# A decoder trunk on one core: the S5 branch's rotations rewritten as reflections in two wide passes

## The chip, the cores and the metric

The kernel runs on one core of a Trainium2 chip. The metric is the device time of one execution in microseconds. Three runs of the kernel before took 1174.33, 1170.13 and 1173.74 us; the median is 1173.74 us. The engines are named as the profile names them: PE is the matrix engine (PEld its weight loads), DVE the vector engine, ACT the scalar engine, POOL the GpSimd engine, SP the engine that issues most of the DMAs.

## The reference, cut to what matters

One layer of a hybrid decoder trunk: one input projection feeds three token mixers (S5, a gated MLP, a gated delta rule), each is gated and projected, the three are merged by sigmoid gates, and one output projection and a LayerNorm follow. The change is in the S5 mixer (and at the seam behind it):

```python
dt = jnp.exp(log_dt)[:, None]
mag = jnp.exp(lr * dt)
ab_r = mag * jnp.cos(li * dt)
ab_i = mag * jnp.sin(li * dt)
...
bu_r = jnp.einsum('gpc,btgc->btgp', bb_r, u)
bu_i = jnp.einsum('gpc,btgc->btgp', bb_i, u)
cum_r, cum_i, s_r, s_i = lax.associative_scan(_cplx_combine, (a_r, a_i, bu_r, bu_i), axis=1)
s_r, s_i = s_r + cum_r * h0r - cum_i * h0i, s_i + cum_r * h0i + cum_i * h0r
y = jnp.einsum('gcp,btgp->btgc', c_re, s_r) - jnp.einsum('gcp,btgp->btgc', c_im, s_i)
z = jax.nn.gelu(y + d * xa)
z = z * jax.nn.sigmoid(z @ w_glu + b_glu)
...
pa = (ya * jax.nn.silu(ga)) @ w_pa
out = (g_a * pa + g_b * pb + g_c * pc) @ w_out
```

There are 64 groups with 64 complex states each, 256 prompt tokens and 8 samples of 4 tokens.

## The kernel before, in words

All activations lie transposed, channels on the 128 partitions and the 288 tokens (256 + 32) along the free axis. A product with a weight tile of 1024x128 is 8 steps of 3 matmuls, since each fp32 operand is split into a high and a low part: a DMA brings `raw` (512 KB), ACT rounds it to `wh` (L201), DVE makes `wl = raw - wh` (the helper `tt`, L136), and PE multiplies high by high, high by low and low by high (L228). Three `raw` buffers rotate. There are 328 such tiles in the program, and they are spread over all stages.

PE's order is written out by hand: products are put in a queue of jobs, and `fill(n)` issues the next n pieces of 12 matmuls between the steps of the mixers. The results land in two PSUM buffers `mm`; a buffer is free again once a `done` function has read it. For a merge gate that reader is a Tanh on ACT into `mth` (L1036) or, for branch A, `mga` (L1063); for the projection that follows it is DVE. The other engines' order is set by the framework's scheduler; each engine runs its own list in that order, so an instruction that waits holds up everything behind it.

The S5 stage (some 365 us) runs 8 blocks of 4 tiles q. A tile is 128 complex states; `TX` is 296, since each of the 8 samples gets one more column for its initial state. For a tile, PE makes `bu` (real and imaginary part), DVE turns it by the phase of each token, a real scan with the magnitude runs over the columns, and DVE turns it back:

- `phases` makes a sine and a cosine table `sn`, `cn` for two tiles at once (one DVE sum `ph`, L1244, and six ACT functions of 512 columns, L1247 to L1251, and four small copies). The pool `s52` gives the tables two buffers, so they cover four tiles.
- `states` makes `am`, the scan's factor, on ACT (L1262, shown as the helper's line L150): a mask times the magnitude. Two buffers rotate. Each of its two turns is two products of 592 columns and two sums of 296.
- POOL copies the initial states into `z` (L1269) between the first turn and the scan (L1271), and the final states out of it (L1278, L1279).
- `turn` copies the input `u` of the next block into the layout for `bu` by 16 small DMAs on SP (`us<-uh`, `us<-ul`, L1222). `us` has one buffer; SP's list has `raw` DMAs among them.

Behind S5 stand the GLU (eight products with `zh`, `zl`), and the projections of branch A (`pa`, operands `yah`, `yal`) in turn with the gate products of branch A, three of which were made ahead.

Of the kernel before, what the change touches and what calls it, by code (L numbers as in the profile page):

```python
# [17 lines left out]
P = 128  # L18
D = 2048
KD = 16  # L20
TP = 256
# [59 lines left out]
LONG = ("ident", "m296", "iota", "iota16", "one", "mean")  # L81
# [3 lines left out]
def constants():  # L85
# [37 lines left out]
    add("mean", np.full((P, P), 1.0 / P))  # L123
# [6 lines left out]
def body(tc, A):  # L130
# [889 lines left out]
    mt3 = tc.alloc_tile_pool(name="mt3", bufs=3, side="right")  # L1020
    s5 = tc.alloc_tile_pool(name="s5", bufs=1, side="right")
# [37 lines left out]
    def merge_gate(m):  # L1059
        def done(ps):  # L1060
            gates[m] = mt3.tile([P, TT], F32, name="mga", tag="mga")
# [129 lines left out]
    class Block:  # L1191


        def __init__(self, n):
# [17 lines left out]
            nc.sync.dma_start(out=self.h0, in_=A["h0"][:, 4 * n:4 * n + 4])  # L1212
            self.cT = s52.tile([P, 4, 2, 32], F32, name="cT", tag="cT")
            nc.sync.dma_start(out=self.cT, in_=A["cT"][:, 4 * n:4 * n + 4])
            ts(self.cT[:, :, 1], self.cT[:, :, 1], -1.0)
            self.s = {}
# [20 lines left out]
        def phases(self, q):  # L1237

            ti = 4 * self.n + q
            ph = s5.tile([P, 2, TP], F32, name="ph", tag="ph")  # L1240
            pk = s5.tile([P, 2, TP], F32, name="pk", tag="pk")
            i0 = fu[:, ti:ti + 2].rearrange("p n (a o) -> p n a o", o=1).to_broadcast([P, 2, 16, 16])
            i1 = fv[:, ti:ti + 2].rearrange("p n (o b) -> p n o b", o=1).to_broadcast([P, 2, 16, 16])
# [10 lines left out]
            self.sn, self.cn = sn, cn  # L1254

        def states(self, q):
            ti = 4 * self.n + q
            bu = self.bu
            cb = mid(self.cn[:, q % 2], 2)
            sb = mid(self.sn[:, q % 2], 2)  # L1260
            am = tmp.tile([P, TX], F32, name="am", tag="s2")
            copy(am, C("m296"), mag[:, ti:ti + 1])  # L1262
# [349 lines left out]
```

## Time and profile before

| | |
|---|---|
| time, median of 3 runs | 1173.74 us |
| the profiled execution: its time, its span | 1173.79 us, 1172.0 us |
| PE busy | 1131.5 us (97%) |
| PEld busy | 1090.1 us (93%) |
| DVE busy | 905.8 us (77%) |
| ACT busy | 614.7 us (52%) |
| POOL busy | 106.7 us (9%) |
| mean granted PE clock | 0.99 |

The span runs from the first to the last instruction; the time holds 1.79 us more around it. Busy is the union of an engine's instructions; the shares are means over stages. In a timeline row the first number is the start in us, the second the duration; an entry in brackets is the idle time of the engine just before it and what ended it. Instructions on DVE overlap a little: where the next one does not depend on the last, it starts some 0.08 us before the last one's end, so the cost of one in a full queue is the distance from start to start.

### The profile page before, as it was taken

What the parts mean: (1) busy time and instruction counts of PE and PEld (TensorE: products, weight loads), DVE (VectorE), ACT (ScalarE), POOL (GpSimd) and SP (SyncE); (2) the same over time, 40 slices, a digit from 0 to 9 for tenths busy, and PEclk for the clock granted to TensorE, in tenths of its full rate; (3) what the DMA queues carried; (4) which work ended last, traced back from release to release, by engine and by line L of the source; (5) the groups of instructions that cost most, each with busy time, mean ns of one, the idle gap of its engine ahead of it and who ended that gap; (6) DMA issues with size and microseconds to landing.
All of it is one profiled execution on the core that took longest, in us unless ns stands there. A gap on an engine that the chain in (4) does not pass through costs nothing.

```text
span 1172.0 us, 25778 instructions
## 1 busy us (share of the span) xinstructions
PE 1131.5 (97%) x10380; PEld 1090.1 (93%) x10380; DVE 905.8 (77%) x1627; ACT 614.7 (52%) x1013; POOL 106.7 (9%) x232
## 2 busy tenths in 40 slices
PE   8999999999999999999999999999999999999995
PEld 7998999999999999999999899989988999999994
DVE  5778757765365989888999999999998755557775
ACT  5665455443363344485666666565653444444553
POOL 0232212100010000000111000000101000000002
PEclk9999999999999999999999999999999999999997
DMA  8553434332375775554545555555455455555552
GB/s 287 173 168 115 146 127 147 136 118 92 126 257 176 249 258 168 179 191 168 185 162 193 162 170 171 162 162 180 151 174 182 156 172 179 179 181 173 181 162 81
DMA packets 65335, 199.24 MB, mean 170 GB/s; under 512 B 10880, under 2 KB 18720, under 8 KB 65088
## 3 DMA queue, kind: packets, MB, share of 16 engines
q1 hardware_dynamic: 63696, 192.12, 49.7%
q0 software_dynamic: 1520, 5.48, 1.2%
q8 instruction: 82, 1.34, 0.5%
q14 instruction: 37, 0.30, 0.1%
HBM read 184.09 MB, written 7.84 MB: 164 GB/s over the span
## 4 chain that ended last, share of the span: by engine, by line
PE 68%; DVE 20%; issue 4%; DMA 4%; ACT 3%; SPq 1%; POOL 0%; DVEq 0%; POOLq 0%; ACTq 0%
PE mm L228 59%; DVE wl L136 7%; DVE z L136 4%; DVE u L136 2%; DVE z L1271 1%; DMA raw<-in_wst 1%; ACT wh L201 1%; PE up L599 1%; PE wp L593 1%; PE a L609 1%; PE y L1288 1%; DMA vu<-in_xT 1%; DMA s<-in_s 1%; DMA cT<-in_cT 1%; DVE ho L136 1%
## 5 line engine op out<-in xcount | busy, mean ns | idle before, releaser
L228 PE MATMUL mm<-xh,wh 128*128 128x288 f32 x1904 | 555.5, 292 | 10.0 <-ACT mth L1036 9.1
L228 PE MATMUL mm<-xh,wl 128*128 128x288 f32 x1904 | 546.0, 287 | 0.9 <-DVE wl L136 0.7
L228 PE MATMUL mm<-xl,wh 128*128 128x288 f32 x1904 | 545.9, 287 | 1.0 <-DVE xl L136 1.0
L136 DVE TENSOR_TENSOR wl<-raw,wh 128x1024 fp32r<-128x1024 f32 x328 | 400.2, 1221 | 160.9 <-ACT wh L201 157.9
L201 ACT CAST wh<-raw 128x1024 fp32r<-128x1024 f32 x328 | 341.3, 1043 | 329.2 <-PE mm L228 288.7
L228 PEld LDWEIGHTS mm<-xh,wh 128*128 128x128 f32 x1904 | 360.9, 190 | 23.8 <-ACT mth L1036 11.8
L228 PEld LDWEIGHTS mm<-xl,wh 128*128 128x128 f32 x1904 | 361.1, 190 | 1.5 <-DVE xl L136 1.2
L228 PEld LDWEIGHTS mm<-xh,wl 128*128 128x128 f32 x1904 | 361.0, 190 | 1.3 <-DVE wl L136 1.3
L228 PE MATMUL mm<-mh,wh 128*128 128x288 f32 x256 | 73.4, 287 | 0.0
L228 PE MATMUL mm<-ml,wh 128*128 128x288 f32 x256 | 73.2, 286 | 0.0
L228 PE MATMUL mm<-mh,wl 128*128 128x288 f32 x256 | 73.2, 286 | 0.0
L136 DVE TENSOR_TENSOR z<-z,u 128x296 f32<-128x296 f32 x128 | 54.9, 461 | 0.6
L1271 DVE TENSOR_TENSOR_SCAN z<-am,z 128x296 f32<-128x296 f32 x64 | 46.9, 764 | 4.4 <-POOL z L1269 2.8
L228 PEld LDWEIGHTS mm<-ml,wh 128*128 128x128 f32 x256 | 48.4, 189 | 0.1
L228 PEld LDWEIGHTS mm<-mh,wh 128*128 128x128 f32 x256 | 48.4, 189 | 0.1
L228 PEld LDWEIGHTS mm<-mh,wl 128*128 128x128 f32 x256 | 48.4, 189 | 0.0
L145 DVE SCALAR_TENSOR_TENSOR cy<-cb,convw,cy 128x312 f32<-128x312 f32 x72 | 38.6, 539 | 6.7 <-ACT cy L367 5.5
L150 ACT ACTIVATE am<-cst,mag 128x296 f32<-128x296 f32 x32 | 17.3, 542 | 47.2 <-DVE z L1271 47.2
L228 PE MATMUL mm<-yah,wh 128*128 128x288 f32 x128 | 36.7, 287 | 0.5 <-DVE yah L1381 0.5
L228 PE MATMUL mm<-ybh,wh 128*128 128x288 f32 x128 | 37.1, 290 | 0.0
L228 PE MATMUL mm<-ych,wh 128*128 128x288 f32 x128 | 37.1, 290 | 0.0
L228 PE MATMUL mm<-ybh,wl 128*128 128x288 f32 x128 | 36.7, 287 | 0.3 <-DVE wl L136 0.3
(435 smaller groups left out, 1656.5 us busy)
## 6 DMA issues: line engine op xcount, KB each, us to landing
raw<-in_wst SPq DMA_DIRECT2D x328, 512.0 KB, 3.3
s<-in_s SPq DMA_DIRECT2D x8, 512.0 KB, 6.5
out_delta_s<-s POOLq DMA_DIRECT2D x8, 512.0 KB, 3.4
us<-uh SPq DMA_DIRECT2D x64, 37.0 KB, 3.2
us<-ul SPq DMA_DIRECT2D x64, 37.0 KB, 3.2
vu<-in_xT SPq DMA_DIRECT2D x3, 576.0 KB, 7.3
out_y<-ho SPq DMA_DIRECT2D x8, 144.0 KB, 2.2
out_y<-ho SPq DMA_DIRECT2D x4, 288.0 KB, 2.5
```

What stands on the lines that cost most here:

```text
L136: (eng or V).tensor_tensor(out=out, in0=a, in1=b, op=op)
L145: V.scalar_tensor_tensor(out=out, in0=a, scalar=s, in1=b, op0=op0, op1=op1)
L150: act(out=out, in_=a, func=AF.Copy, scale=scale)
L201: S.copy(out=h, in_=r)
L228: T.matmul(pairs(ps), lhsT=w, rhs=paired(x), start=start, stop=stop)
L593: T.matmul(wp[R, h4], lhsT=xt[R, h4], rhs=r[R, h4], start=True, stop=True)
L599: T.matmul(up[:, h4], lhsT=kd[R, h4], rhs=w[R, h4], start=True, stop=True)
L609: T.matmul(a[Q, h4], lhsT=nb[R, h4, 1], rhs=w[R, h4], start=(c == 0 and h4 == 0), stop=True, skip_group_check=True)
L1271: V.tensor_tensor_scan(out=z[:, ri], data0=am, data1=z[:, ri], initial=0.0, op0=mult, op1=add)
L1288: T.matmul(self.y5[32 * q:32 * q + 32, 0:TX], lhsT=self.cT[:, q, ri], rhs=self.s[q][:, ri], start=(ri == 0), stop=(ri == 1), tile_position ...
```

## The change

- `phases` makes the tables of one tile: a sum `pk` of 256 columns, and a table `tab` with three rows: cosine, sine, minus cosine. On ACT it is two functions of 256 columns, two of 512 (both angles at once), a third Sin of 256 and one copy of 120 columns. `tab` has three buffers (pool `s53`), and `phases` is called for every tile.
- `reflect` makes both parts of a turn in two instructions: one product `pr` of 1184 columns (both parts of x, each times two neighbouring rows of `tab`), and one sum of 592. As rows (cosine, sine) and (sine, minus cosine) this is a reflection, which is its own inverse: the scan runs on the conjugate, so the imaginary part of the initial state `h0` is negated once per block (8 new small DVE instructions), and the same function turns back.
- `am` is made on POOL.
- One gate product (`merge_gate(3)`) is queued between the GLU and the first `pa`, with the pool `mt6` of six buffers for the gates from the fourth on; the gates run four ahead.
- The constant `mean` (128 columns) is gone; `one` and a scale of 1/128 in the copy take its place.

```diff
         def phases(self, q):
...
-            ph = s5.tile([P, 2, TP], F32, name="ph", tag="ph")
             pk = s5.tile([P, 2, TP], F32, name="pk", tag="pk")
-            tt(ph.rearrange("p n (a b) -> p n a b", a=16), i0, i1, add)
-            sn = s52.tile([P, 2, TX], F32, name="sn", tag="sn")
-            cn = s52.tile([P, 2, TX], F32, name="cn", tag="cn")
-            act(out=pk, in_=ph, func=AF.Abs, bias=hp[:, 1:2])
-            act(out=ph, in_=ph, func=AF.Abs)
-            for a_, tb in ((pk, sn), (ph, cn)):
-                act(out=a_, in_=a_, func=AF.Abs, bias=hp[:, 2:3])
-                act(out=tb[:, :, 0:TP], in_=a_, func=AF.Sin, scale=TURN, bias=hp[:, 3:4])
-                for i in range(2):
-                    copy(tb[:, i, TP:].rearrange("p (b t) -> p b t", t=5), mid(tb[:, i, 0:5], 8))
+            tt(pk[:, 0].rearrange("p (a b) -> p a b", a=16), i0, i1, add)
+            tab = s53.tile([P, 3, TX], F32, name="tab", tag="tab")
+            act(out=pk[:, 1], in_=pk[:, 0], func=AF.Abs, bias=hp[:, 1:2])
+            act(out=pk[:, 0], in_=pk[:, 0], func=AF.Abs)
+            act(out=pk, in_=pk, func=AF.Abs, bias=hp[:, 2:3])
+            act(out=tab[:, 0:2, 0:TP], in_=pk, func=AF.Sin, scale=TURN, bias=hp[:, 3:4])
+            act(out=tab[:, 2, 0:TP], in_=pk[:, 0], func=AF.Sin, scale=-TURN, bias=hp[:, 0:1])
+            first5 = tab[:, :, 0:5].rearrange("p k (o t) -> p k o t", o=1).to_broadcast([P, 3, 8, 5])
+            copy(tab[:, :, TP:].rearrange("p k (b t) -> p k b t", t=5), first5)
+            self.turns[q] = bass.AP(tensor=tab.tensor, offset=tab.offset, ap=[list(tab.ap[0]), [TX, 2], [TX, 2], [1, TX]])
+
+        def reflect(self, z, x, q):
+            pr = s5.tile([P, 2, 2, TX], F32, name="pr", tag="pr")
+            xb = x.rearrange("p i (o t) -> p i o t", o=1).to_broadcast([P, 2, 2, TX])
+            tt(pr, xb, self.turns[q], mult)
+            tt(z, pr[:, 0], pr[:, 1], add)

         def states(self, q):
...
-            copy(am, C("m296"), mag[:, ti:ti + 1])
+            ts(am, C("m296"), mag[:, ti:ti + 1], eng=G)
             z = s53.tile([P, 2, TX], F32, name="z", tag="z")
-            u = s5.tile([P, 2, TX], F32, name="u", tag="u")
-            tt(z, bu[:, :, 0:TX], cb, mult)
-            tt(u, bu[:, :, 0:TX], sb, mult)
-            tt(z[:, 0], z[:, 0], u[:, 1], add)
-            tt(z[:, 1], z[:, 1], u[:, 0], sub)
+            self.reflect(z, self.bu[:, :, 0:TX], q)
...
-            u = s5.tile([P, 2, TX], F32, name="u", tag="u")
-            tt(u, z, sb, mult)
-            tt(z, z, cb, mult)
-            tt(z[:, 0], z[:, 0], u[:, 1], sub)
-            tt(z[:, 1], z[:, 1], u[:, 0], add)
+            self.reflect(z, z, q)
...
-            if q == 1:
-                B.phases(2)
-            elif q == 3 and nxt:
+            if q < 3:
+                B.phases(q + 1)
+            elif nxt:
                 nxt.phases(0)
...
+    mtg.append(tc.alloc_tile_pool(name="mt6", bufs=6, side="right"))
+    merge_gate(3)
     for m in range(16):
         merge_a(m)
-        if m < 13:
-            merge_gate(m + 3)
+        if m < 12:
+            merge_gate(m + 4)
```

PE's list is the same but for one gate product (48 matmuls), which stands between the last `zh` and the first `yah` product, and the later ones that shift with it.

On DVE, the second tile of the first block, from the product that reads `bu` on (`wl` is the weight stream's instruction, `merged` a merge of another branch), before:

```order
L136 TENSOR_TENSOR z<-bu,cn 128x592
L136 TENSOR_TENSOR u<-bu,sn 128x592
L136 TENSOR_TENSOR wl<-raw,wh 128x1024
L136 TENSOR_TENSOR z<-z,u 128x296 x2
L145 SCALAR_TENSOR_TENSOR merged<-mth,mm 128x288
L1271 SCALAR_TENSOR_TENSOR z<-am,z 128x296 x2
L136 TENSOR_TENSOR wl<-raw,wh 128x1024
L136 TENSOR_TENSOR u<-z,sn 128x592
L136 TENSOR_TENSOR z<-z,cn 128x592
L136 TENSOR_TENSOR z<-z,u 128x296
L136 TENSOR_TENSOR wl<-raw,wh 128x1024
L136 TENSOR_TENSOR z<-z,u 128x296
```

The same tile on DVE now (the scan is the row with `am`):

```order
L135 TENSOR_TENSOR pr<-bu,tab 128x1184
L135 TENSOR_TENSOR wl<-raw,wh 128x1024
L135 TENSOR_TENSOR z<-pr 128x592
L144 SCALAR_TENSOR_TENSOR merged<-mth,mm 128x288
L1271 SCALAR_TENSOR_TENSOR z<-am,z 128x296 x2
L135 TENSOR_TENSOR wl<-raw,wh 128x1024
L135 TENSOR_TENSOR pr<-z,tab 128x1184
L135 TENSOR_TENSOR z<-pr 128x592
```

Eight instructions of a tile's two turns have become four; the weight stream's place among them is the same.

On ACT, in the fourth block, from the copies of `turn` to the next gate's Tanh `mth`, which frees a PSUM buffer of PE, before:

```order
L1230 CAST ws<-wtp 128x512
L1205 COPY w_6471<-bh 64x16x16 x2
L150 ACTIVATE am<-cst_143,mag 128x296
L201 CAST wh<-raw 128x1024
L1251 ACTIVATE sn<-pk,hp 128x2x256
L1251 ACTIVATE cn<-ph,hp 128x2x256
L150 ACTIVATE sn<-sn 128x40 x2
L150 ACTIVATE cn<-cn 128x40 x2
L1199 CAST bh<-bb 128x128
L201 CAST wh<-raw 128x1024
L1036 ACTIVATE mth<-mm,bgate 128x288
```

The same place on ACT now:

```order
L1231 CAST ws<-wtp 128x512
L1205 COPY w_6471<-bh 64x16x16 x2
L200 CAST wh<-raw 128x1024
L1249 ACTIVATE tab<-pk,hp 128x2x256
L1250 ACTIVATE tab<-pk,hp 128x256
L149 ACTIVATE tab<-tab 128x3x40
L200 CAST wh<-raw 128x1024
L1036 ACTIVATE mth<-mm,bgate 128x288
```

`am` is gone from the way to `mth`, and the first instruction here that needs a buffer back from DVE is the first `tab`.

On POOL, one tile's instructions now (before, the second of these rows did not exist):

```order
L1269 COPY z<-h_7477 128x2x8
L139 TENSOR_SCALAR am<-cst_143,mag 128x296
L1273 COPY sst<-z 128x2
L1274 COPY sst<-z 128x2x8
L1269 COPY z<-h_7477 128x2x8
```

Each `am` is made for the tile two ahead, so it waits for the scan of the tile whose initial states were copied just before it; the copies of the final states stand behind it.

## Rows read from the trace of the kernel before

**Rows 1.** Busy time by stage: us, PE, PEld, DVE, ACT, POOL, clock, DMA
```profile
540.00:905.00 365.00, 353.53 (x2813) 336.97 (x2812) 354.90 (x559) 218.73 (x371) 38.16 (x97) 1.00 0.52 169
905.00:945.00 40.00, 37.73 (x288) 36.89 (x288) 28.14 (x51) 16.66 (x24) 0.00 (x0) 0.96 0.49 162
```

**Rows 2.** PE's waits from 540 to 945 us: total, times, longest
```profile
PE mm L228 <- ACT mth L1036: 8.7, 9, 1.8
PE bu L228 <- DMA us<-ul: 2.6, 1, 2.6
...
PE mm L228 <- DVE yah L1381: 0.5, 1, 0.5
```

**Rows 3.** ACT's longest wait in the S5 stage
```profile
ACT am L150 <- DVE z L1271: 47.2, 26, 5.9
```

**Rows 4.** ACT's timeline before one of PE's waits: start, duration, instruction
```profile
667.04 0.54 ACT L150 ACTIVATE am<-cst,mag 128x296 f32<-128x296 f32 x1 [2.44 <-DVE z L1271]
...
668.42 0.72 ACT L1251 ACTIVATE sn<-pk,hp 128x512 f32<-128x512 f32 x1
...
670.67 1.04 ACT L201 CAST wh<-raw 128x1024 fp32r<-128x1024 f32 x1
671.62 0.49 ACT L1036 ACTIVATE mth<-mm,bgate 128x288 f32<-128x288 f32 x1
```

**Rows 5.** PE's timeline, the wait that this ended
```profile
672.16 0.39 PE L228 MATMUL mm<-xh,wh 128*128 128x288 f32 x1 [1.30 <-ACT mth L1036]
```

**Rows 6.** DVE's groups in the S5 stage: count, busy us, mean ns
```profile
L136 DVE TENSOR_TENSOR z<-z,u 128x296 f32<-128x296 f32 x128 | 54.9, 461 | 0.6
...
L136 DVE TENSOR_TENSOR z<-bu,cn 128x592 f32<-128x592 f32 x32 | 24.6, 768 | 0.1
```

**Rows 7.** DVE's timeline, a stretch without idle time
```profile
603.50 0.46 DVE L136 TENSOR_TENSOR z<-z,u 128x296 f32<-128x296 f32 x1
603.88 0.69 DVE L136 TENSOR_TENSOR ph<-fu,fv 128x512 f32<-128x512 f32 x1
604.48 1.22 DVE L136 TENSOR_TENSOR wl<-raw,wh 128x1024 fp32r<-128x1024 f32 x1
605.62 0.77 DVE L136 TENSOR_TENSOR z<-bu,cn 128x592 f32<-128x592 f32 x1
606.30 0.77 DVE L136 TENSOR_TENSOR u<-bu,sn 128x592 f32<-128x592 f32 x1
607.10 0.47 DVE L136 TENSOR_TENSOR z<-z,u 128x296 f32<-128x296 f32 x1
```

**Rows 8.** ACT's groups in the S5 stage: `am` and a table function
```profile
L150 ACT ACTIVATE am<-cst,mag 128x296 f32<-128x296 f32 x30 | 16.3, 542 | 47.2 <-DVE z L1271 47.2
...
L1251 ACT ACTIVATE sn<-pk,hp 128x512 f32<-128x512 f32 x14 | 10.1, 721 | 4.6 <-DVE u L136 4.4
```

**Rows 9.** POOL's timeline at the last tile of S5
```profile
902.00 1.12 POOL L1278 COPY sst<-z 128x2 f32<-128x2 f32 x1 [5.04 <-DVE z L136]
903.06 0.20 POOL L1279 COPY sst<-z 128x16 f32<-128x16 f32 x1
```

**Rows 10.** DVE's timeline at the same place
```profile
901.86 1.22 DVE L136 TENSOR_TENSOR wl<-raw,wh 128x1024 fp32r<-128x1024 f32 x1
```

**Rows 11.** POOL's groups over the whole span: its widest elementwise work
```profile
L136 POOL TENSOR_TENSOR ho<-ho,rsb 128x288 f32<-128x288 f32 x4 | 3.5, 912 | 253.8 <-ACT rsb L150 253.8
```

**Rows 12.** DVE's waits in the S5 stage: the one on POOL
```profile
DVE z L1271 <- POOL z L1269: 2.8, 7, 0.4
```

**Rows 13.** SP's timeline at the last block's `turn`
```profile
845.23 1.15 SPq L1222 DMA_DIRECT2D us<-uh  x2
848.17 0.33 SPq L196 DMA_DIRECT2D raw<-in_wst  x1
848.55 1.53 SPq L1222 DMA_DIRECT2D us<-ul  x2
```

**Rows 14.** Busy time by stage, the five us in which PE waits for that `us`
```profile
850.00:855.00 5.00, 2.55 (x11) 2.58 (x12) 4.90 (x9) 1.65 (x3) 1.05 (x1) 0.69 0.67 221
```

More of the change, by code (lines that the diff above doesn't have):

```diff
@@ L77, in weight_order @@
     return o
-LONG = ("ident", "m296", "iota", "iota16", "one", "mean")
+LONG = ("ident", "m296", "iota", "iota16", "one")
 _CW = {}
@@ L122, in constants @@
     add("one", np.ones((P, P)))
-    add("mean", np.full((P, P), 1.0 / P))
     return [np.ascontiguousarray(np.concatenate(x, 1)) for x in parts]
@@ L1020, in body @@
     mt3 = tc.alloc_tile_pool(name="mt3", bufs=3, side="right")
+    mtg = [mt3]
     s5 = tc.alloc_tile_pool(name="s5", bufs=1, side="right")
@@ L1060, in done @@
         def done(ps):
-            gates[m] = mt3.tile([P, TT], F32, name="mga", tag="mga")
+            gates[m] = mtg[m > 2].tile([P, TT], F32, name="mga", tag="mga")
             with tc.high_priority():
@@ L1212, in __init__ @@
             nc.sync.dma_start(out=self.h0, in_=A["h0"][:, 4 * n:4 * n + 4])
+            ts(self.h0[:, :, 1], self.h0[:, :, 1], -1.0)
             self.cT = s52.tile([P, 4, 2, 32], F32, name="cT", tag="cT")
@@ L1215, in __init__ @@
             ts(self.cT[:, :, 1], self.cT[:, :, 1], -1.0)
-            self.s = {}
+            self.s, self.turns = {}, {}
         def turn(self):
@@ L1239, in phases @@
             ti = 4 * self.n + q
-            ph = s5.tile([P, 2, TP], F32, name="ph", tag="ph")
             pk = s5.tile([P, 2, TP], F32, name="pk", tag="pk")
-            i0 = fu[:, ti:ti + 2].rearrange("p n (a o) -> p n a o", o=1).to_broadcast([P, 2, 16, 16])
-            i1 = fv[:, ti:ti + 2].rearrange("p n (o b) -> p n o b", o=1).to_broadcast([P, 2, 16, 16])
-            tt(ph.rearrange("p n (a b) -> p n a b", a=16), i0, i1, add)
-            sn = s52.tile([P, 2, TX], F32, name="sn", tag="sn")
@@ L1254, in phases @@
-            self.sn, self.cn = sn, cn
+            i0 = fu[:, ti].rearrange("p (a o) -> p a o", o=1).to_broadcast([P, 16, 16])
+            i1 = fv[:, ti].rearrange("p (o b) -> p o b", o=1).to_broadcast([P, 16, 16])
+            tt(pk[:, 0].rearrange("p (a b) -> p a b", a=16), i0, i1, add)
[3 more added lines that the diff above has]
+            act(out=pk, in_=pk, func=AF.Abs, bias=hp[:, 2:3])
@@ L1397, in merge_a @@
         queue([(("pa", m, 0), lambda k: yah[:, k], lambda k: yal[:, k])], done)
+    mtg.append(tc.alloc_tile_pool(name="mt6", bufs=6, side="right"))
+    merge_gate(3)
     for m in range(16):
         merge_a(m)
-        if m < 13:
-            merge_gate(m + 3)
+        if m < 12:
+            merge_gate(m + 4)
     drain()
+    mtg[1].release()
     mt3.release()
@@ L1454, in body @@
     sh = psl.tile([P, 512], F32, name="sh", tag="sh")
-    T.matmul(sh[:, 0:TT], lhsT=C("mean"), rhs=ho[:, 0], start=True, stop=True)
-    copy(shift, sh[:, 0:TT])
+    T.matmul(sh[:, 0:TT], lhsT=C("one"), rhs=ho[:, 0], start=True, stop=True)
+    copy(shift, sh[:, 0:TT], 1.0 / P)
     tt(ho[:, 0], ho[:, 0], shift, sub)
```

3 lines of the change are left out of this document (removed).

## Prediction

> **What bounds the kernel now.** I read the table of busy time by stage first, then who waited for whom, then the timelines around the longest waits. In the table the reader is to see that the S5 stage, 540 to 905 us, has two nearly full engines: PE 353.5 and DVE 354.9 of 365 us [rows 1]. Neither is full by itself; each loses about 11 us to the other. The stage cannot fall below PE's 353.5, since the change takes no matmul out. So the whole prize here is PE's idle time of 11.5 us, and what the clock loses beside it.
>
> PE's waits say where that time lies: 8.7 us in nine waits for `mth`, the Tanh on ACT that frees a PSUM buffer, and 2.6 us once for a small DMA of `us` [rows 2]. ACT is only 219 us busy [rows 1], so why is it late? Its longest wait is `am`, 47.2 us in 26 waits for DVE's scan [rows 3]: `am` has two buffers, and ACT's list stops there until DVE has done the scan two tiles back. One case in full: `am` starts at 667.04 after waiting 2.44 us, then come `wh`, two table functions, copies and `wh` again, and `mth` starts at 671.62 [rows 4]; PE, idle for 1.30 us by then, goes on at 672.16 [rows 5]. The chain is DVE late, ACT held, PE held. A microsecond taken from DVE's list comes back on PE as long as such waits are left, and no longer.
>
> **The change part by part.** *The turns.* Before, a tile has four products of 592 columns and four sums of 296 on DVE; the groups count 128 sums, and 32 of each product [rows 6]. Their busy means, 461 and 768 ns, overstate the cost, because neighbours overlap. From start to start, in a stretch without idle time, 296 columns took 0.38 us (603.50 to 603.88), 512 took 0.60, 1024 took 1.14 and 592 took 0.68 [rows 7]. The line through 296 and 1024 is 0.071 us + 1.044 ns a column; it gives 0.69 for 592 and 1.31 for the new 1184. One turn was 2 x 0.69 + 2 x 0.38 = 2.14 us and becomes 1.31 + 0.69 = 2.00: the columns are the same, only two fixed costs go. 64 turns give 9.1 us. If instead the busy means counted in full (1184 by the same slope 1.39 us), a turn would save 2 x 0.461 + 2 x 0.768 - 1.39 - 0.77 = 0.30, and 64 turns 19 us: the upper end. The lower end is none: the sum depends on the product just before it, and where no other instruction stands between, a dependent one starts 0.80 us after a 592 product (606.30 to 607.10) where an independent one starts after 0.68 [rows 7]; 0.12 a turn would eat nearly all of the 0.14.
>
> *The tables.* DVE now makes 32 sums of 256 columns (0.34 by the line, 10.8 us) for 16 of 512 (9.6 us): 1.2 us more. The negated `h0` is 8 instructions of 32 columns, 0.1 us each by the line, 0.8 us. Net relief of DVE: 9.1 - 1.2 - 0.8 = 7.1 us; between -2 and +17.
>
> *ACT.* From `am`'s 542 ns for 296 columns and 721 ns for 512 [rows 8], 0.83 ns a column and 0.30 us fixed: 0.51 for 256, 0.40 for 120, 0.33 for 40. A tile had three functions of 512, two small copies and `am`: 3.36 us. Now it is two of 512, three of 256 and one of 120: 3.37 us. ACT's load stays. What holds it up moves: `am` no longer stops it, but `tab` has three buffers for three tiles where `sn` and `cn` covered four, so the first `tab` of a tile waits until DVE's second product three tiles back has read its own. In the order that product is a `wl` and a product behind the scan, 1.14 + 1.31 = 2.45 us later; from there to `mth` stand 0.72, 0.51, 0.40 and a `wh` of 1.04, less some overlap, 2.3 us. Together 4.75 us from the scan's end to `mth`, against 4.58 from `am` to `mth` before [rows 4]. So ACT's path gains nothing, and the relief is DVE's alone.
>
> *`am` on POOL.* No row shows this instruction. A POOL copy of 16 columns took 0.20 us [rows 9], a two-operand instruction of 288 columns 0.91 us [rows 11]; `am` lies between, nearer the middle, 0.5 us. What does it cost DVE? POOL's copy at 902.00 took 1.12 us and ended as DVE's `wl` (901.86, 1.22 us) ended, while its twin right after took 0.20 [rows 9, 10]: POOL is shut out while DVE reads two operands from SBUF. The other way round DVE would be shut out by `am`. Bounds: 0, and 32 x 0.91 = 29.2 us. I take 1.0 us. `am` becomes ready when the scan ends, and DVE goes straight on with two-operand work, so POOL has to wait; the next instructions that read PSUM are a merge and `pr<-bu`, and the latter's 1.31 us hold an `am` and the two copies behind it, 0.5 + 2 x 0.2. The row nearest to it: 96 POOL copies in this stage cost DVE 2.8 us [rows 12], and most of that is the copy that the scan waits for in any case. Nothing waits for a late `am` until the scan two tiles on.
>
> The Trainium skill speaks against this edit: "SBUF — State Buffer", section "Who interferes with whom", makes the port pair that DVE and GpSimd share an exclusive lock, held for a whole instruction by whichever came first. The trace agrees for one direction, with the 1.12 us above; which direction `am` meets, no run here shows. The Trainium skill gives `am` a price too: its "GPSIMD Engine Reference", section "3.1 Elementwise — side-by-side cycle accounting", has 512 one-input elements in 769 ns, by which 296 would be an estimated 0.44 us; if each of the 32 held DVE for that long, 14 us would be lost, and the sum below would be about 1180.
>
> *The transfer of `us`.* At the last block's `turn` a `raw` DMA stands between the two pairs of `us` copies; it went out at 848.17, 1.8 us after SP was free, and the second pair at 848.55 [rows 13]. PE waited 2.65 us and then ran at a granted 0.69, between its levels of 1.2 and 2.4 GHz; in those five us it did 2.55 x 0.69 = 1.8 us of full-speed work [rows 14], so 3.2 us went. The order there is the same now. `raw` waits for a `wl` on DVE; I let the wait shrink by DVE's relief in one block, 0.6 us.
>
> *The gate product before `pa`.* It covers the 0.5 us wait for `yah` [rows 2]; behind it, four instead of three projections follow each other at the end, each with 24 matmuls, and DVE is at 28 of 40 us around the seam [rows 1]: free of cost. The constant `mean` saves a piece of one DMA, nothing on PE's path.
>
> **Sum.** The profiled execution took 1173.79 us, span 1172.0, and agrees with the median 1173.74. DVE's relief 7.1 - 1.0 = 6.1, below the 8.7 that it can pay back; `us` 0.6; `yah` 0.5: 7.2 us less, **1166.6 us**.
>
> **Rivals.** *The lock turns the sign.* Each `am` gets hold of the shared ports between two DVE instructions and DVE stands still for it. It decides from 7.1 / 32 = 0.22 us a tile on; at 0.5 us the 32 tiles cost 16, DVE's list is 8.9 us longer in a stage that it nearly fills, and with 0.5 for `yah` the time is 1182; at 0.91 us, 1195. For it: POOL's two-operand 288 columns do take 0.91 us. Against it: the order, by which POOL is the one that comes second. *The wait only moves.* `tab` stops ACT at the same distance from `mth` as `am` did, with a buffer less in depth, and a DVE that is 2% lighter is still held by its own bursts: the nine waits stay, and only `yah`'s 0.5 goes: 1173.3. For it speak the 4.75 against 4.58 us. *All of it goes.* DVE falls so far below PE that it is early everywhere: 8.7 + 3.2 + 0.5 us less, 1161.4. For it: DVE's 354.9 would be 348.8 against PE's 353.5, the first clear gap between them; against it: bursts, and `raw` in the same place. *The dependent sum eats the saving*: with nothing between product and sum the turns save almost nothing and DVE loses 2 us on the tables: 1175, told with the second rival.
>
> **How the numbers follow.** My forecast has 0.40, spread over 1163 to 1170; all goes 0.17; the wait only moves (or the sum eats it) 0.29; the lock 0.14. About 0.5%, 5.9 us, is what a measurement of this kernel can tell from no change: below 1167.9 is faster, above 1179.6 slower. Faster: 0.17 + 0.33 = 0.50; same: 0.29 + 0.07 = 0.36; slower 0.14. The range for 8 in 10 leaves out the worse part of the lock and the best of the gain: 1159 to 1177.
>
> **What would show it.** After the change, DVE's two turns should be groups of 64 products near 1.39 us and 64 sums near 0.77 us, with DVE's busy time in S5 six to nine us lower. PE's waits for `mth` should be some 3 us in total, with ACT's first waits at `tab`, not `am`; the `yah` wait gone. `am` on POOL should be long where DVE's `wl` runs and end with it. The forecast is wrong if DVE's rows show idle time or stretched two-operand instructions beside `am`, if PE's waits for `mth` stay at 8 us or more, or if a new wait for `us` shows at other blocks.

## The result and the profile after

The changed kernel took 1178.97 us (median of 5 runs, 1177.62 to 1182.04) beside 1173.01 us for the kernel before (5 runs): a ratio of 1.0057 [1.0042, 1.0072]. The forecast was 1166.6 with a range up to 1177, so it is wrong in sign, and the range misses. A ratio, here and below, is taken over runs in the faster of the two states in which executions fall; it need not be the quotient of two medians. The profiled execution has a span of 1175.9 us (before 1172.0) and a granted clock of 0.99 in the mean.

The same two stages by the clock on the wall, answering [rows 1]:

```profile
540.00:905.00 365.00, 346.46 (x2741) 328.04 (x2740) 345.49 (x446) 224.95 (x372) 127.72 (x124) 1.00 0.49 165
905.00:945.00 40.00, 38.49 (x310) 37.19 (x309) 29.97 (x50) 17.52 (x25) 1.87 (x3) 1.00 0.50 173
```

DVE is busy 9.4 us less in that window, but that is not its relief: PE has done less too, 346.5 against 353.5 us, since the window ends before the stage does. A fairer cut runs from PE's first `bu` product to its last `y` product, so that each kernel is measured over the same work. Before, after, and the fastest experiment (told below), one row each:

```profile
540.21:903.23 363.02, 351.55 (x2799) 335.73 (x2797) 354.19 (x558) 217.09 (x370) 37.56 (x96) 1.00 0.52 169
```

```profile
537.44:909.78 372.34, 353.81 (x2800) 335.10 (x2800) 352.01 (x451) 227.16 (x375) 129.32 (x127) 1.00 0.49 165
```

```profile
538.45:895.34 356.89, 350.33 (x2799) 334.44 (x2797) 346.99 (x452) 243.95 (x415) 57.56 (x97) 1.00 0.53 173
```

S5 became 372.34 - 363.02 = 9.3 us longer: PE is idle 18.5 instead of 11.5 us, and the same matmuls took 2.3 us more. Over the same work DVE is busy only 2.2 us less (352.0 against 354.2), where the prediction looked for six to nine. From the last `y` to the merge behind branch A the changed kernel is 3.2 us shorter, and it comes to S5 2.8 us earlier, though the code ahead of it is the same. Only about 1.1 us of this is the change (see `seam_only` below): in the profiled execution of before the granted clock was 0.50, the level of 1.2 GHz, from 909.9 to 913.3 us, behind two waits of PE for `zh` and `zl`, and in the other runs S5 starts anywhere between 536.2 and 540.5 us. PE's waits, to be held against [rows 2]:

```profile
PE mm L227 <- ACT mth L1036: 7.2, 7, 2.0
PE wtp L1230 <- ACT ws L1231: 5.9, 3, 2.9
PE bu L227 <- DMA us<-ul: 3.3, 3, 1.8
PE mm L227 <- DVE wl L135: 1.7, 4, 1.0
```

`mth` has hardly fallen from 8.7, `yah` is gone, and a wait is there that before did not have: at three block boundaries the transposes of `turn` (`wtp`) stand still until ACT has copied the first half (`ws`) away. Of the 7 us that PE stands longer, `ws` is the largest part. ACT's and DVE's waits in S5:

```profile
ACT tab L1249 <- DVE pr L135: 48.4, 19, 4.3
...
ACT pk L1246 <- DVE pk L135: 30.5, 19, 3.8
```

```profile
DVE wl L135 <- ACT wh L200: 10.4, 10, 1.9
DVE pk L135 <- ACT tab L1250: 3.6, 2, 1.8
```

The 47.2 us at `am` [rows 3] have become 48.4 at `tab`, and the wait for the phase sum has grown from 13.9 to 30.5 us. DVE in turn waits twice as long for `wh` (5.4 before). These two, before:

```profile
ACT pk L1247 <- DVE ph L136: 13.9, 8, 2.6
```

```profile
DVE wl L136 <- ACT wh L201: 5.4, 5, 1.6
```

One case in full, the end of the fifth block: ACT, then DVE, then PE.

```profile
754.20 0.51 ACT L1246 ACTIVATE pk<-pk,hp 128x256 f32<-128x256 f32 x1 [1.93 <-DVE pk L135]
...
756.58 0.49 ACT L1250 ACTIVATE tab<-pk,hp 128x256 f32<-128x256 f32 x1
757.11 0.30 ACT L149 ACTIVATE tab<-tab 128x120 f32<-128x120 f32 x1
757.57 0.51 ACT L1246 ACTIVATE pk<-pk,hp 128x256 f32<-128x256 f32 x1 [0.16 <-DVE pk L135]
757.98 0.48 ACT L1036 ACTIVATE mth<-mm,bgate 128x288 f32<-128x288 f32 x1
758.36 1.03 ACT L200 CAST wh<-raw 128x1024 fp32r<-128x1024 f32 x1
759.30 0.58 ACT L1231 CAST ws<-wtp 128x512 fp32r<-128x512 f32 x1
```

```profile
752.60 1.22 DVE L135 TENSOR_TENSOR wl<-raw,wh 128x1024 fp32r<-128x1024 f32 x1
753.74 0.43 DVE L135 TENSOR_TENSOR pk<-fu,fv 128x256 f32<-128x256 f32 x1
754.09 1.21 DVE L135 TENSOR_TENSOR wl<-raw,wh 128x1024 fp32r<-128x1024 f32 x1
757.11 0.43 DVE L135 TENSOR_TENSOR pk<-fu,fv 128x256 f32<-128x256 f32 x1 [1.80 <-ACT tab L1250]
...
780.77 1.38 DVE L135 TENSOR_TENSOR pr<-bu,tab 128x1184 f32<-128x1184 f32 x1
```

```profile
759.94 0.66 PE L1230 MATMUL wtp<-cst,w 128*128 128x128 f32 x4 [2.89 <-ACT ws L1231]
```

ACT stops 1.93 us for a sum that DVE has behind a `wl`; it makes the table; the next sum of DVE waits 1.80 us because `pk` has one buffer and ACT is still reading it; ACT stops again for that sum; `mth`, `wh` and `ws` come late, and PE stands 2.89 us. The table over which all this happened was ready at 757.41 and read first at 780.77, 23 us later. Over all 32 tiles a table is ready 24.7 us ahead of its first reader in the mean, 15.6 at the least.

DVE's turns [rows 6] and POOL's new instruction:

```profile
L135 DVE TENSOR_TENSOR z<-pr 128x592 f32<-128x592 f32 x63 | 50.2, 797 | 0.4
...
L135 DVE TENSOR_TENSOR pr<-z,tab 128x1184 f32<-128x1184 f32 x32 | 45.0, 1408 | 0.4
L135 DVE TENSOR_TENSOR pr<-bu,tab 128x1184 f32<-128x1184 f32 x31 | 42.8, 1381 | 0.1
```

```profile
L139 POOL TENSOR_SCALAR am<-cst,mag 128x296 f32<-128x296 f32 x30 | 80.5, 2682 | 59.3 <-DVE z L1271 57.7 <-DVE h L139 1.6
```

### The profile page after: what moved, and what is told of

Same layout as the page of the kernel before. It is cut to its first block, busy times and chain, and to the rows that moved or that the text cites. A ratio compares the mean times of both kernels' runs of the same rounds, so it can differ in the third digit from the quotient of the medians.

```text
span 1175.9 us, 25783 instructions
## 1 busy us (share of the span) xinstructions
PE 1131.8 (96%) x10380; PEld 1087.6 (92%) x10380; DVE 903.5 (77%) x1523; ACT 623.1 (53%) x1013; POOL 200.8 (17%) x264
## 4 chain that ended last, share of the span: by engine, by line
PE 70%; DVE 17%; issue 5%; ACT 4%; DMA 2%; POOL 1%; SPq 0%; DVEq 0%; POOLq 0%; ACTq 0%
PE mm L227 60%; DVE wl L135 5%; DVE pr L135 3%; DVE z L1271 2%; DVE z L135 2%; ACT wh L200 2%; POOL z L1269 1%; PE up L598 1%; PE wp L592 1%; PE a L608 1%; PE y L1283 1%; DMA s<-in_s 1%; DMA raw<-in_wst 1%; DMA vu<-in_xT 1%; DVE ho L135 1%
## 5 line engine op out<-in xcount | busy, mean ns | idle before, releaser
L139 POOL TENSOR_SCALAR am<-cst,mag 128x296 f32<-128x296 f32 x32 | 84.1, 2628 | 75.7 <-DVE z L1271 57.7
L135 DVE TENSOR_TENSOR z<-pr 128x592 f32<-128x592 f32 x64 | 51.0, 797 | 0.4
L1249 ACT ACTIVATE tab<-pk,hp 128x512 f32<-128x512 f32 x32 | 23.1, 723 | 50.4 <-DVE pr L135 48.4
L1269 POOL COPY z<-h 128x16 f32<-128x16 f32 x32 | 18.4, 574 | 183.7 <-DVE z L135 158.8
L227 PEld LDWEIGHTS mm<-mh,wh 128*128 128x128 f32 x256 | 48.4, 189 | 0.1
L227 PEld LDWEIGHTS mm<-ml,wh 128*128 128x128 f32 x256 | 48.4, 189 | 0.1
L227 PEld LDWEIGHTS mm<-mh,wl 128*128 128x128 f32 x256 | 48.4, 189 | 0.0
L135 POOL TENSOR_TENSOR ho<-ho,rsb 128x288 f32<-128x288 f32 x4 | 3.6, 912 | 251.7 <-ACT rsb L149 251.7
L135 DVE TENSOR_TENSOR pr<-z,tab 128x1184 f32<-128x1184 f32 x32 | 45.0, 1408 | 0.4
L135 DVE TENSOR_TENSOR pr<-bu,tab 128x1184 f32<-128x1184 f32 x32 | 44.2, 1382 | 0.1
```

The source lines that it names most:

```text
L135: (eng or V).tensor_tensor(out=out, in0=a, in1=b, op=op)
L139: (eng or V).tensor_scalar(out=out, in0=a, scalar1=s1, scalar2=None, op0=op0)
L227: T.matmul(pairs(ps), lhsT=w, rhs=paired(x), start=start, stop=stop)
L1249: act(out=tab[:, 0:2, 0:TP], in_=pk, func=AF.Sin, scale=TURN, bias=hp[:, 3:4])
L1269: G.tensor_copy(out=z[:, :, TP:].rearrange("p r (b t) -> p r b t", t=5)[:, :, :, 0], in_=self.h0[:, q])
```

## The experiments

All ratios are to the kernel before, run on the same chip, with 95% intervals, from 5 to 12 runs each. "The changed kernel" is 1.0057. In the words on record, theory A says that ACT and DVE hold each other up.

### am on POOL

`am_act`: the changed kernel with `copy(am, C("m296"), mag[:, ti:ti + 1])` (ACT) for `ts(am, ..., eng=G)` (POOL).

> The changed kernel with one part undone: am is made on ACT again. Theory A (ACT and DVE wait for each other at the one-tile tables): ACT's list gets a second wait on DVE per tile back and 17 us more work, so the time stays or rises, 1178 to 1184 us, and PE's waits on ACT stay at 13 us or more. Theory B (am on POOL shuts DVE out of SBUF): the 23 stretched DVE instructions (4.9 us in all) are gone and the time falls by about that, to 1174 us or below.

1178.67 us, 1.0059 [1.0040, 1.0078]. No gain; S5 as long as in the changed kernel. ACT's longest wait is `am` again, 40.2 us: what POOL no longer costs, this stop seems to cost instead (see `am_both` and `am_act_am_pinned`).

`no_am`: the changed kernel with `am = C("m296")`, no instruction for `am` at all.

> The changed kernel without am: the scan takes the mask itself as its factor, so the magnitude is left out of the states and POOL makes no am. Nothing else moves by hand. Theory A: little changes, 1176 to 1180 us, since the waits at tab and pk stay. Theory B: all of the loss was POOL's; DVE's 4.9 us of stretch go and the time falls to 1172 us or below.

1175.76 us, 1.0036 [1.0023, 1.0049]. Of the 0.57%, 0.21 go with `am` on POOL, hardly more than the intervals allow; 0.36 stay.

`am_pool_only`: the kernel before, `am` moved to POOL, nothing else.

> The kernel before with one part of the change: am on POOL. Theory A: ACT loses its longest wait (47 us) and 17 us of work while the tables stay two tiles wide and four deep, so PE's 8.7 us of waits for mth shrink: 1167 to 1172 us. Theory B: some 5 us of stretched DVE instructions come in and nothing else: 1176 to 1179 us.

1178.79 us, 1.0053 [1.0034, 1.0072]. This is theory B's number, and its stretched DVE instructions are there (26 beside `am`, 5.3 us in all). Theory A, which had a relief of ACT here, missed: the wait moved to `sn` (30.4 us) and the edit by itself lost 6 us. Two causes are possible, POOL's contention and the new order of ACT's list, so:

`am_both`: the kernel before, and POOL does an idle twin.

```diff
             copy(am, C("m296"), mag[:, ti:ti + 1])
+            spare = s5.tile([P, TX], F32, name="spare", tag="spare")
+            ts(spare, am, mag[:, ti:ti + 1], eng=G)
```

> The kernel before, with POOL doing an instruction like the moved am for nothing: each tile POOL multiplies am by the magnitude into a spare tile that nobody reads (128x296), while ACT makes am as before; the lists of all other engines are the same as before, instruction for instruction. It tells POOL's contention with DVE from the changed order. If the contention makes the 0.53% that am on POOL cost in the kernel before: 1175 to 1179 us, DVE's two-operand instructions beside it stretched by 0.2 us each. If the order of the lists makes it (ACT without am runs into sn): 1171 to 1173.

1174.93 us, 1.0035 [1.0020, 1.0050]: 4.1 us with all other lists unchanged. Contention makes about two thirds of the loss of `am_pool_only`, with wide intervals. The profiled execution of this run (span 1171.2) is no longer than that of before, but its S5 is, by 3.4 us (366.41 against 363.02); it is shorter ahead of S5 and behind it, where the code is the same.

```profile
537.89:904.30 366.41, 351.99 (x2798) 334.80 (x2797) 359.00 (x558) 216.69 (x370) 92.96 (x126) 1.00 0.52 167
```

```profile
PE mm L228 <- ACT mth L1036: 10.9, 10, 2.1
```

DVE is busy 359.0 instead of 354.2 us for the same instructions (25 of them are stretched beside the twin, by 4.9 us), and PE's wait for `mth` grew from 8.7 to 10.9 us.

### The seam alone

`seam_only`: the kernel before with `merge_gate(3)` and `mt6`.

> The kernel before with one part of the change: one gate product between GLU and projection, and the mt6 pool. The PE's wait for yah (0.5 us) and the slots around it go: 1171 to 1172.5 us by both theories; if the seam was part of the loss, above 1175.

1170.86 us, 0.9991 [0.9979, 1.0003]: by its time 1 us at most likely, not told apart from none. The profiles tell it apart: from the end of the last `y` to the end of the last merge of branch A it took 150.2 to 150.3 us in all nine runs with this product, and 151.3 to 151.6 in nine of the eleven without; the other two, before among them, had a stretch at half clock there. That is 1.1 us.

### The turns and the tables, each alone

`wide_pairs`: the kernel before, with one wide product per turn and two narrow sums (sine and cosine lie in one tile; the constant `mean` is gone, as in the change, and `one` is a column).

```diff
...
-            tt(z, bu[:, :, 0:TX], cb, mult)
-            tt(u, bu[:, :, 0:TX], sb, mult)
-            tt(z[:, 0], z[:, 0], u[:, 1], add)
-            tt(z[:, 1], z[:, 1], u[:, 0], sub)
+            pr = products(bu[:, :, 0:TX])
+            tt(z[:, 0], pr[:, 0, 0], pr[:, 1, 1], add)
+            tt(z[:, 1], pr[:, 1, 0], pr[:, 0, 1], sub)
...
```

> The kernel before with one thing of the change: each turn makes its four products in one instruction of 1184 columns, and two sums of 296 follow; the tables stay those of before (two tiles at once, sine and cosine now in one tile, four tiles deep), am stays on ACT. From the start-to-start line of the trace a turn falls from 2.14 to 1.31 + 2 x 0.38 = 2.07 us, 64 turns save 4.5 us of DVE. Theory A (the change loses by its tables: made for one tile, three buffers, so that ACT and DVE wait for each other at every tile; the turns themselves only save): 1167 to 1171 us, DVE's idle time in S5 stays near 9 us, ACT's waits stay am and sn. Theory B (the wide product itself does harm, because it lies longer ahead of the scan and of the weight stream's wl, and DVE's longer steps hold ACT and PE up): 1174 to 1178, with more idle time on DVE and more waits for wh.

1172.02 us, 1.0007 [0.9996, 1.0017]. The turns' steps on DVE, from start to start and without the waits behind them, fell from 141.0 to 135.6 us (4.5 reckoned), and in S5 DVE's idle time rose by as much, from 363.0 - 354.2 = 8.8 to 363.7 - 349.6 = 14.1 us:

```profile
536.76:900.45 363.69, 351.30 (x2798) 334.65 (x2796) 349.59 (x494) 218.35 (x370) 45.53 (x96) 1.00 0.52 169
```

Neither theory's number: the shape does no harm, and the relief alone gives nothing.

`one_tile_3` and `one_tile_4`: the kernel before with tables for one tile, three and four buffers (the old turns).

```diff
...
-            sn = s52.tile([P, 2, TX], F32, name="sn", tag="sn")
+            sn = s54.tile([P, TX], F32, name="sn", tag="sn")
...
-            if q == 1:
-                B.phases(2)
+            if q < 3:
+                B.phases(q + 1)
```

> The kernel before with the other thing alone: the tables sn and cn are made for one tile at a time, with three buffers, and phases runs for every tile; turns (eight instructions) and am (ACT) as before. Work added: 16 sums on DVE (1.2 us) and about 32 x 0.9 us of fixed costs on ACT, whose load is far from full. Theory A: the change's loss is here, 1175 to 1179 us, ACT waits at the first table function and for the phase sum some 30 us each, DVE's idle time in S5 rises from 8.7 to 15 us or more, PE waits for ws appear. Theory B: 1171 to 1174, no more idle time.

1179.60 us, 1.0070 [1.0057, 1.0083]. The tables alone lose more than the whole change, and PE's and ACT's waits look like those of the changed kernel:

```profile
PE mm L228 <- ACT mth L1036: 10.3, 10, 2.6
PE wtp L1230 <- ACT ws L1231: 5.0, 3, 2.9
...
ACT pk L1248 <- DVE ph L136: 27.3, 18, 3.2
```

Of the two waits of some 30 us that theory A had, only the one for the sum came; at `sn` it was 5.4 us.

> The same as the kernel with one-tile tables, with four table buffers instead of three, so that the tables again cover four tiles as in the kernel before. If the depth is what costs (theory A with the buffers as its cause): 1171 to 1173 us, and ACT's waits at the first table function fall by most. If the meeting of DVE's phase sum and ACT at every tile costs, whatever the depth (A with the hand-over as its cause): as with three buffers, within 1 us, with ACT's waits for the phase sum unchanged.

1181.48 us, 1.0087 [1.0073, 1.0102]. A fourth buffer does not help. It makes the tables 35.3 us early instead of 24.4, and ACT's waits stay (29.2 us for the sum). Depth, which the prediction had feared, is not the cause here; with the reflections, where 48.4 us go at `tab` for a buffer, four were not tried.

`pair_sum_4`: as `one_tile_4`, but DVE's phase sum for two tiles at once.

> As the kernel with one-tile tables and four buffers (1.0087 of before), but DVE's phase sum is made for two tiles at once again, 16 times 512 columns; ACT's functions stay those of one tile at a time, so ACT's load stays (32 x 6 functions of 256, some 0.9 us a tile above before). Theory D (what costs is how often ACT stops in its list for DVE's phase sum, 18 waits and 29 us there against 8 and 14 in the kernel before): the time falls back by more than half, to 1172 to 1175 us, ACT's waits for the phase sum near 14 us. Theory E (what costs is ACT's work for the tables, more and shorter functions): it stays at 1179 to 1182.

1175.02 us, 1.0036 [1.0024, 1.0048]. Of 0.87%, 0.51 are gone with half of the phase sums, with ACT's work the same; the wait for the sum is 12.1 us, and PE's wait for `ws` 1.7 instead of 4.8. What holds the other 0.36% was not told apart; ACT's more and shorter functions (theory E) may.

### Stops taken away

`before_no_am` (the scan takes the mask) and `before_one_table` (calls of `phases` in the loop left out): ACT's stops out of the kernel before, one kind at a time.

> The kernel before without am: the scan takes the mask alone, the magnitude is left out. It shows what the best form of one edit of the change is worth by itself: ACT does not stop for the scan, and no other engine makes am. If am's wait (47.2 us on ACT) is what made mth late: 1163 to 1167 us, with PE's waits for mth at 3 us or less. If the wait only moves to the next instruction that needs DVE (sn, as it did when am was made on POOL): 1170 to 1173, with some 30 us at sn on ACT. If it is 1174 or more, am's wait had kept ACT and DVE in a better order, and its removal does harm without any POOL.

1170.94 us, 1.0002 [0.9991, 1.0013]; 30.2 us of wait moved to `sn`.

> The kernel before with no tables inside the loop: the first two tiles' tables serve all tiles (the other phases are left out), turns and am as before. DVE loses 15 sums of 512 (0.60 us each, 9 us), ACT 45 functions of 512 and the small copies (some 40 us). Theory D: ACT's stops for the tables (13.9 us for the sum, 7 for the tables in the kernel before) go, the stop at am stays: 1166 to 1171 us. If ACT's stops are not what makes mth late (theory F: PE's waits come from the burst of work at the block boundaries): 1171 to 1174.

1172.14 us, 1.0004 [0.9992, 1.0017]; `am`'s wait grew to 87.0 us. Taking away one stop lengthens the other. The number lies outside theory D's range and inside theory F's; but F, the bursts at the block boundaries, is not borne out: `before_all_pinned` below has the same work there and 0.2 us of waits for `mth`.

`after_one_table`: the same calls left out of the changed kernel.

> The changed kernel with no tables inside the loop: the first tile's table serves all tiles (the other phases are left out); reflections, am on POOL and the seam as in the changed kernel. Theory D (the tables for one tile at a time are what lost the time, the wide turns cost nothing by themselves): the loss goes; what is left of it is am on POOL, so within 0.4% of the kernel before without tables, 1167 to 1173 us; ACT's longest wait is no longer for DVE, and PE's waits for ws are gone. If the wide turns or the list that they make hold things up in their own right: 1174 or more.

1162.24 us, 0.9922 [0.9910, 0.9935], far better than expected: no stop of ACT for DVE's tables or scan is left, and the forecast's picture of PE comes true.

```profile
PE mm L227 <- ACT mth L1036: 2.8, 4, 1.1
PE bu L227 <- DMA us<-ul: 1.8, 1, 1.8
...
ACT wh L200 <- PE mm L227: 123.4, 70, 3.9
```

ACT's longest wait is now for PE's weight buffers: it runs ahead, as it should. Beside `before_one_table`, where the same calls are left out, the change is now worth 0.8%. That is the turns' relief with `am` off ACT, which stopped there for 87.0 us, and the seam; the run does not part them. With its tables made in the loop the kernel loses all of it and more.

### The same instructions in other places

`after_pinned`: in the changed kernel a tile's first table function may not be scheduled ahead of any ACT instruction that the program writes before it.

```diff
-            act(out=pk[:, 1], in_=pk[:, 0], func=AF.Abs, bias=hp[:, 1:2])
+            tc.keep_in_program_order(act(out=pk[:, 1], in_=pk[:, 0], func=AF.Abs, bias=hp[:, 1:2]))
```

> The changed kernel with one thing moved: the first table function of a tile may not stand in ACT's list ahead of any ACT instruction that the program writes before it. Instructions, buffers and data are the same; only places in the lists differ. In the changed kernel a table is ready 24.7 us (mean of 32 tiles, least 15.6) before DVE's first product reads it: ACT stops for tables that nobody needs yet. Theory H (ACT stops because the table functions stand too early in its list, where DVE has not yet got to; the late place takes the stops away): ACT's waits for the phase sum and for tab's buffer fall from 79 us by more than half, PE's waits for ws go, and the time is 1164 to 1171 us. Theory G (one meeting of ACT and DVE for each tile costs the same wherever it stands): 1176 to 1181.

1169.13 us, 0.9979 [0.9969, 0.9989]: 0.78% less than the changed kernel, with not one instruction more or less. PE's and POOL's lists are the same; the scheduler also moved DVE's phase sums, and some 70 of DVE's other 1491 instructions (some 230 in `all_pinned` beside `am_act`), so what moved are places in two lists, ACT's and DVE's. The tables are now 6.3 us early (least 0.6); `tab`'s wait is gone, 25.6 us for the sum are left, and PE's wait for `ws` is gone.

`am_act_tab_pinned`: the same edit in `am_act`.

> The changed kernel with am back on ACT (1.0059 of before) and the table functions moved as in the run with pinned tables. Theory H: as there, and better by what am on POOL costs (0.2 to 0.35%) less what ACT's stop for am costs: 1163 to 1172. Theory G: 1176 to 1181.

1177.31 us, 1.0050 [1.0033, 1.0068]: the number of theory G, but not for its reason. Here the instruction before the pinned one is `am`, itself free to move ahead, so the pin moved little: the first function stands right behind an `am` 15 times (3 in `am_act`), and tables stay 23.4 us early. So the run does not test theory H.

`am_act_am_pinned`: `am_act` with only `am` pinned (the same wrapper).

> The changed kernel with am on ACT, and am alone pinned; the table functions may float to the front as before. With the tables pinned and am free it was 1.005, with both pinned 0.9917 (but there the pin of the tables stood behind a free am, and so moved nothing). Theory H for the tables: 1175 to 1180 us, ACT's waits at tab and pk near 60 us or more. If am was the stop that mattered, and the tables are innocent where am is late: 1160 to 1166.

1170.41 us, 0.9990 [0.9980, 1.0000]. `am`'s wait is gone, and 0.7% with it; it is ready 6.0 us before its scan, where it was 22.7 in `am_act`. Of the tables (24.3 us early) the waits stay: neither of the two expectations, both kinds of stop cost.

```profile
PE wtp L1230 <- ACT ws L1231: 4.9, 3, 2.5
...
ACT tab L1249 <- DVE pr L135: 44.7, 21, 3.8
```

`all_pinned`: `am_act` with both pinned.

> As the run before this one, and am too may not stand ahead of an ACT instruction that the program writes before it; so ACT reaches am when the scan of two tiles back is long done. Theory H, with am as one more stop of the same kind: ACT's wait for am falls from 40 us to under 15, PE's waits for mth to 4 us or less, and the time is 1160 to 1168, the best of all. If a late place only makes the scan wait for am instead: DVE waits for am appear, and it is 1172 or more.

1161.95 us, 0.9917 [0.9901, 0.9932], the fastest of those that leave nothing out, 1.4% below `am_act`. The tables are 5.8 us early (least 0.35):

```profile
PE mm L227 <- DVE wl L135: 3.2, 4, 2.0
PE bu L227 <- DMA us<-ul: 2.5, 2, 1.6
...
PE mm L227 <- ACT mth L1036: 0.6, 1, 0.6
...
ACT pk L1246 <- DVE pk L135: 13.9, 12, 2.9
```

The waits for `mth` are down to 0.6 us, those for `am`, `tab` and `ws` are gone from the list, and DVE never waits for a table.

`before_pinned` (tables) and `before_all_pinned` (tables and `am`): the places without the change.

> The kernel before with its table functions (two tiles at once) pinned in the same way, nothing else. It tells what the place alone is worth without the reflections. Its DVE is busy for 354 of the 363 us of the stage, so theory H gives little: 1168 to 1172 us. If it gains 8 us or more, the place alone does it and the reflections add nothing to a run with pinned tables.

1170.27 us, 0.9991 [0.9981, 1.0001]; the pin, behind a free `am`, moved the tables by 2.7 us only (from 23.4 to 20.7 ahead of their first reader).

> The kernel before with both its table functions and am pinned, as in the fastest run so far (0.9917 of before), but without the reflections, the one-tile tables and the seam. It tells whether the places alone make that time. Theory H with DVE as the second bound (the stage holds 354 us of DVE's work in 363, so taking ACT's stops away gives little until the reflections lighten DVE; the same was seen without tables, 1.0004): 1166 to 1171 us. If the places alone do it: 1160 to 1164.

1170.47 us, 0.9985 [0.9972, 0.9998]. Here `mth` holds PE for 0.2 us only, and yet S5 is only 2.2 us shorter than the 363.0 of before. The stage in one row, and PE's waits:

```profile
539.05:899.82 360.77, 352.23 (x2803) 336.31 (x2802) 354.45 (x559) 222.50 (x385) 48.19 (x95) 1.00 0.52 170
```

```profile
PE bu L228 <- DMA us<-ul: 6.3, 3, 2.7
...
PE mm L228 <- ACT mth L1036: 0.2, 1, 0.2
```

DVE is busy 354.5 of 360.8 us; with ACT out of the way it is DVE, and the transfer of `us`, that set the end. Of PE's 8.5 us of idle time `us` takes 6.3, and DVE is behind it. In the longest case SP's list stood at a `raw` for DVE's `wl`, which ended at 844.02; the `us` copies behind that `raw` came late, and PE, idle for 2.66 us, went on at 848.24:

```profile
842.81 1.21 DVE L136 TENSOR_TENSOR wl<-raw,wh 128x1024 fp32r<-128x1024 f32 x1
```

```profile
844.05 0.33 SPq L196 DMA_DIRECT2D raw<-in_wst  x1
844.43 0.51 SPq L1222 DMA_DIRECT2D us<-uh  x1
```

Places alone give 0.15%; the change with `am` on ACT (reflections, tables for one tile, seam) alone loses 0.59%; both together gain 0.83%.

## Why the prediction was wrong

**The step that failed** is the one on ACT: "So ACT's path gains nothing, and the relief is DVE's alone." I compared one path to `mth`, 4.75 against 4.58 us, called it a wash, and let ACT's part of the sum be nothing. But ACT's list also carries `wh` and `ws`, and the path to `ws` is not in the prediction: there PE now stands 5.9 us, where before it never waited. The meetings of ACT with DVE for a table had doubled, to a sum and a buffer for each tile instead of one of each for two tiles, and ACT's stops at the tables went from 20.8 to 80.6 us, while 47.2 us at `am` went away. With the old turns and `am` on ACT, the tables alone cost 0.70% (`one_tile_3`, 8.2 us); half of the sums gave more than half of the loss back (`pair_sum_4`). In the changed kernel the price of the places is 0.78% (`after_pinned`). I had the depth of the buffers as the danger, but the tables were 24.7 us early: they stopped ACT because they stood too early, not because they came late. The lead of a table over its first reader could have been read from the trace of before (there, 23.4 us); I did not look.

Neither the number of ACT's stops for DVE nor their sum orders the runs: with `am` counted in, they are 45 in 68.0 us before and 39 in 80.6 in the changed kernel, but 52 in 66.7 in `am_act`, which loses as much, and 63 in 79.6 in `pair_sum_4`, which loses less than half of what `one_tile_4` does (61 in 82.8). PE's wait for `ws` follows the tables better: 4.0 to 5.9 us in all seven runs that make a sum for each tile and have the tables early, 1.7 in `pair_sum_4`, none in the others. That a stop costs by the urgent instruction that stands behind it is argued from cases like the one shown, not counted. The parts do not add up either: 8.2 us for the tables, 2.5 for `am` on POOL and -1.1 for the seam would be 9.6, and 6.7 were measured (1.0057).

**The frame, "a microsecond taken from DVE's list comes back on PE as long as such waits are left",** fell too. `wide_pairs` took 5 us from DVE and got none; `before_all_pinned` took nearly all of the `mth` wait from PE and got 2.2 us in S5. The reading that fits is that before, ACT's stops and DVE's load each held the stage at nearly the same length, so either relief alone shows nothing. It is not isolated: `all_pinned` has the one-tile tables and the seam as well, and no run joined `wide_pairs` with later places.

**The turns** were right: 9.1 us reckoned, and from start to start, without the waits behind them, the steps of the turns fell from 141.0 to 132.5 us, 8.5, and to 130.2 with `am` back on ACT (`am_act`). The dependent sum did not eat it. The tables on DVE (reckoned at 1.2 us) cost a little more: counted in the same way, 28 sums for one tile took 10.5 us in S5 where 13 for two tiles took 8.4, some 1.7 us for all. Of the relief, 4.8 us went back into instructions that were stretched beside `am` (next).

**am on POOL** was mis-sized: 1.0 us in the sum, 2.5 (`no_am`: 1.0057 - 1.0036) to 4.1 (`am_both`) measured. The direction was right: POOL is the one shut out, with 2682 ns in the mean for what took 1.03 us where it was shortest (0.5 was reckoned). But 23 of DVE's instructions beside it were stretched too, by 0.21 us in the mean, 4.8 us in all. Beside the `am` that ran from 543.55 to 546.75:

```profile
545.86 1.00 DVE L135 TENSOR_TENSOR z<-pr 128x592 f32<-128x592 f32 x1
```

It takes 0.77 alone. The Trainium skill, "SBUF — State Buffer", section "Who interferes with whom", says that a DVE instruction with two SBUF inputs contends with a GpSimd instruction that reads SBUF. The trace agrees, on few cases: of some 96 such instructions that ran beside an `am`, 23 were stretched (`wl`, `pr<-z`, `z<-pr` and `w<-bb`), and none of the 11 with an input in PSUM, two `pr<-bu` and nine merges. DVE was never held for as long as an `am` took, as the prediction's lock would have it.

**`us`** did not shrink: 3.3 us in three waits against 2.6 in one, where 0.6 less was reckoned; waits at other blocks were one of the signs of being wrong. The clock was misread there: the 0.69 of [rows 14] is the mean of two us at full clock, in which PE stood, and three at 0.50 (1.2 GHz), in which it worked, so the work was 2.55 x 0.50 = 1.3 us, and 3.7 us went, not 3.2.

```profile
852.00:855.00 3.00, 2.55 (x11) 2.58 (x12) 3.00 (x6) 1.65 (x3) 0.00 (x0) 0.50 0.72 224
```

**The seam** was right: the `yah` wait is gone, and 1.1 us were gained where 0.5 was reckoned.

**The rivals.** "The wait only moves" named the place, `tab` for `am`, with 48.4 for 47.2 us, but gave 1173.3, as if a moved wait cost what the old one did; it brought a second kind of stop with it. "The lock" has the sign, but not the size: DVE was stretched by 4.8 / 32 = 0.15 us a tile, less than the 0.22 from which on it decides. "All of it goes", 1161.4, is close to what the change does with `am` on ACT and both in later places, 1161.95; that the numbers meet so closely is chance, since 2.5 us of waits for `us` and 3.2 for `wl` are left there, and the kernel before took 1171.58 beside it.

**Left open:** why the same matmuls of S5 took 2.3 us more in the changed kernel, with a granted clock of 1.00 throughout; how much DVE's new order adds to what the later places give; and how much of the wait at `pk` (13.9 us in the fastest run) could still be removed.

## What to carry to other kernels

When an edit cuts a step into smaller ones, look at the meetings between engines that it adds: each is a place where one in-order list can stop with unrelated urgent work behind it, and what stands behind it mattered more than how many there were, as far as these runs tell. Read for each produced tile how long it lies ready before its first reader; where that is long and its maker waits, a later place in the list may be worth more than another buffer, as it was here. Before paying for relief on one engine, ask by a run that takes out the other engine's stops whether two bounds lie at the same length, since then each edit alone may measure as nothing and only both together show.

## What was not expected of the hardware

- A POOL instruction on 128x296 took 1.03 to 4.16 us (mean 2.68) beside DVE's two-operand work, and 1.79 in the mean as the idle twin beside the kernel before; DVE paid 0.21 us in the mean on 23 of its instructions, and 25 with 4.9 us in all beside the twin.
- The same list of instructions, in other places, differed by 1.4% (1178.67 against 1161.95 us) with PE's matmuls unchanged; besides its idle time, PE's busy time for the stage's same matmuls moved by 5 us, 350.3 to 355.2. In the slower run PE worked 6.0 us at a granted clock of 0.50 (1.2 GHz), after it had stood 2.88 us for `ws`; half of that, 3.0 of the 5 us, is the clock's. In the changed kernel a wait of 2.89 us at the same place was followed by no fall.

```profile
759.40:766.20 6.80, 6.03 (x26) 6.03 (x27) 6.14 (x8) 4.41 (x9) 0.21 (x1) 0.50 0.37 112
```
